# Linear attention on one core: two more groups' stores issued from SyncE instead of GpSimd

## The chip, the core and the metric

The kernel runs on one core of a Trainium2 chip. A core has TensorE (PE in the profile, with its weight loads as PEld), VectorE (DVE), ScalarE (ACT), GpSimd (POOL) and SyncE (SP), and sixteen DMA engines that carry out transfers between HBM and the core's SBUF. A transfer is issued by an instruction on one of the engines; here SP and POOL do it. The metric is the device time of one execution in microseconds, and the median over several executions is compared.

## What is computed

Q, K and V have the shape 8 × 12 × 512 × 64, in float32; the output has the same shape.

```python
Q_feat = np.maximum(0, Q) + 1
K_feat = np.maximum(0, K) + 1
KV = np.einsum('bhkd,bhkv->bhdv', K_feat, V)
K_sum = np.sum(K_feat, axis=2)
numerator = np.einsum('bhqd,bhdv->bhqv', Q_feat, KV)
denominator = np.einsum('bhqd,bhd->bhq', Q_feat, K_sum)
return numerator / (denominator[:, :, :, None] + 1e-10)
```

Each input is 12.58 MB, and so is the output. There are 96 heads; each has a 64 × 64 matrix KV and a vector K_sum.

## The kernel before

The 96 heads are cut into `NG` = 12 groups of eight heads. One group is 1 MB of each input in float32 and 1 MB of output. Loads convert to bfloat16 as they are written to SBUF (except the very first K load)[...]: one load per tensor for two groups at a time (`load_pair`, L105), except that the first and last two groups are loaded singly.

A group passes through these steps: `k_features` and `q_features` (VectorE), `v_blocks` (copies of V into a block layout, three on VectorE and one on ScalarE), `keys_values` (32 matmuls, then casts on ScalarE), `transposes` (16 on TensorE, copies on ScalarE), `output` (32 matmuls in two halves `h`, then on VectorE a reciprocal, L199, and a multiplication, L200, which writes `o_sb`), and `store` (L112). `o_sb` comes from a pool of `OUT_BUFS` = 6 buffers, so output 10 writes the buffer that store 4 reads, and output 11 that of store 5.

The order of the instructions on each engine is the order of the program text (`tc.manual_schedule`, L218). The loop of L234 runs over groups 0 to 10. In the turn of group g, VectorE prepares g, TensorE works on groups g−1, g−2 and g in turn, after odd groups the next loads are issued on POOL, and at the turn's end stands the store of group g − 3 (`LAG`, L16). So the loop issues stores 0 to 7. Behind the loop comes the rest of the work on the last groups, with outputs 9, 10 and 11, and at the very end (L257) the stores 8 to 11.

Before the change the stores of groups 0 to 9 are issued on POOL, one transfer of 1 MB each (L116). The stores of groups 10 and 11 are issued on SP, each as two transfers of 512 KB (L119), one for each half `h` that `output` writes. A transfer waits, on the engine that issues it, for the VectorE instructions that write its data. Apart from the four halves, SP issues one transfer only, the first load of K, at the start (L90).

Of the kernel before, what the change touches and what calls it, by code (L numbers as in the profile page):

```python
# [19 lines left out]
def kernel(  # L20
# [18 lines left out]
    nc = tc.nc  # L39
# [7 lines left out]
    NG = NPAIR // NP  # L47
# [64 lines left out]
    def store(g):  # L112
        o_sb = outs.pop(g)
        o_to = o_dram[:, g * NP : g * NP + NP]
        if g < NG - 2:
            nc.gpsimd.dma_start(out=o_to, in_=o_sb)  # L116
            return
        for h in range(2):
            nc.sync.dma_start(out=o_to[:, h:NP:2], in_=o_sb[:, h:NP:2])  # L119
# [98 lines left out]
    with tc.manual_schedule():  # L218
# [15 lines left out]
        for g in range(NG - 1):  # L234
            k_features(g)
            v_blocks(g)
            q_features(g)
            if g:
                transposes(g - 1)
            if g >= 2:  # L240
                output(g - 2)
            keys_values(g)
            if g % 2 and g // 2 + 2 < NG // 2:
                load_pair(g // 2 + 2)
            if g >= LAG:
                store(g - LAG)
# [10 lines left out]
        for g in range(last - LAG, NG):  # L257
            store(g)
# [30 lines left out]
```

## Time and profile before

| | |
|---|---|
| median of 8 runs | 127.59 us (127.2 to 128.22) |
| profiled execution | 127.59 us |
| its span, from the first to the last instruction | 125.8 us |
| busy: PE, DVE, ACT, POOL | 65.2, 88.1, 68.0, 27.8 us |
| granted TensorE clock, mean | 0.84 |
| stores issued on POOL | 10 of 1 MB |
| stores issued on SP | 4 of 512 KB |
| last VectorE instruction ends | 120.8 us |

Times in the profile are counted from the start of the span. In its rows, an arrow `out<-in` names the tile that is written and the one that is read, `xN` a count, and L116 a line of the kernel. The queue q0 (`software_dynamic`) holds the transfers issued on POOL, q1 (`hardware_dynamic`) those issued on SP; q8 and q14 are instruction fetches. Issuing a transfer is not the transfer: the profile shows the issue as an instruction, and separately when the transfer landed, as a semaphore that each of the sixteen DMA engines raises when its share is done. A share of the DMA queues can be a little over 100%, since an engine's packets overlap.

### The profile page before, as it was taken

The page shows a single profiled execution, that of the slowest core. Times are in us where ns is not written, and L with a number is a line of the kernel's source. Part 1 is how long each engine was busy: PE and PEld are TensorE (multiplying, and loading weights), DVE is VectorE, ACT ScalarE, POOL GpSimd, SP SyncE. Part 2 cuts the span into 40 slices and gives each one's busy share as a digit, 9 for nine tenths or more (in the row PEclk, how much of TensorE's full clock was granted, in tenths as well). Part 3 has the DMA queues.
Part 4 walks back from the last instruction along what each step waited for, and adds up shares of the span by engine and source line. Part 5 has one row for each costly group of instructions (what it writes and reads, how often), then busy time and mean ns, then how long its engine had stood idle before and what let it go on. Part 6 is the DMA issues. An engine that isn't in the chain of part 4 may idle for free.

```text
span 125.8 us, 2337 instructions
## 1 busy us (share of the span) xinstructions
PE 65.2 (52%) x960; PEld 48.4 (38%) x960; DVE 88.1 (70%) x188; ACT 68.0 (54%) x87; POOL 27.8 (22%) x43
## 2 busy tenths in 40 slices
PE   0005938000059785696929486004987659695500
PEld 0003636000046564574817364003656536483300
DVE  4896280206199799999989990519969999667930
ACT  7841396007600789729893962580069880988000
POOL 6990222000002082022800241202420202020000
PEclk9999999855555999679999999955589976999955
DMA  3999999999999999999999999999999999999992
GB/s 95 328 212 210 212 204 208 212 209 212 214 210 212 213 211 213 212 212 216 249 415 289 186 214 210 212 354 389 221 210 210 216 272 415 418 419 406 400 387 108
DMA packets 13419, 32.13 MB, mean 255 GB/s; under 512 B 608, under 2 KB 608, under 8 KB 13408
## 3 DMA queue, kind: packets, MB, share of 16 engines
q0 software_dynamic: 12048, 28.84, 98.5%
q1 hardware_dynamic: 1360, 3.15, 6.7%
q8 instruction: 7, 0.11, 0.3%
q14 instruction: 4, 0.03, 0.1%
HBM read 37.75 MB, written 12.58 MB: 400 GB/s over the span
## 4 chain that ended last, share of the span: by engine, by line
DMA 40%; DVE 26%; PE 17%; POOL 6%; issue 6%; DVEq 0%; POOLq 0%
DMA q_raw<-in_Q_dram 40%; DVE o_sb L200 15%; PE kva_ps L157 11%; DVE v_all L140 4%; PE qt_ps L176 3%; DVE recip L199 3%; PE o_ps L189 3%; POOL v_raw L99 2%; DVE qf L122 2%; DVE kf L122 2%; POOL q_raw L99 1%; POOL kva_diag L231 1%; POOL k_raw L99 1%; POOL identity masks.py:199 0%; POOL identity masks.py:197 0%
## 5 line engine op out<-in xcount | busy, mean ns | idle before, releaser
L157 PE MATMUL kva_ps<-v_all,kf 128*64 128x320 bf16 x384 | 36.4, 356 | 12.9 <-DVE v_all L140 12.9
L189 PE MATMUL o_ps<-kva_diag,qt 128*64 128x130 bf16 x384 | 19.3, 236 | 41.5 <-DVE o_sb L200 41.0
L140 DVE COPY v_all<-v_raw 32x2048 bf16<-32x2048 bf16 x36 | 26.4, 733 | 11.7 <-DMA v_raw<-in_V_dram 11.3
L200 DVE TENSOR_TENSOR o_sb<-o_ps,recip 128x512 f32<-128x512 f32 x48 | 33.2, 691 | 1.6
L157 PEld LDWEIGHTS <-kf 128*64 128x64 bf16 x384 | 25.4, 133 | 20.6 <-DVE v_all L140 13.1
L189 PEld LDWEIGHTS <-qt 128*64 128x64 bf16 x384 | 12.8, 115 | 47.1 <-DVE o_sb L200 45.3
L138 ACT COPY v_all<-v_raw 32x2048 bf16<-32x2048 bf16 x12 | 22.7, 1894 | 13.8 <-DMA v_raw<-in_V_dram 13.6
L177 ACT COPY qt<-qt_ps 128x1024 bf16<-128x1024 bf16 x24 | 29.7, 1310 | 0.3
L167 ACT CAST kva_diag<-kva_ps 64x256 bf16<-64x256 f32 x24 | 8.9, 371 | 33.2 <-PE kva_ps L157 33.0
L99 POOL DMA_DIRECT2D k_raw<-in_K_dram x7 | 5.3, 754 | 38.7 <-DVE kf L122 37.0
L122 DVE TENSOR_SCALAR qf<-q_raw 128x1024 bf16<-128x1024 bf16 x24 | 9.1, 422 | 6.4 <-DMA q_raw<-in_Q_dram 6.2
L116 POOL DMA_DIRECT2D out_dram<-o_sb x10 | 8.5, 849 | 22.3 <-DVE o_sb L200 13.0
L199 DVE RECIPROCAL recip<-o_ps 128x8 f32<-128x8 f32 x48 | 9.5, 198 | 4.9 <-PE o_ps L189 4.8
L122 DVE TENSOR_SCALAR kf<-k_raw 128x1024 bf16<-128x1024 bf16 x22 | 8.7, 437 | 6.0 <-DMA k_raw<-in_K_dram 6.0
L176 PE MATMUL qt_ps<-identity,qf 128*128 128x128 bf16 x192 | 12.8, 220 | 0.0
L176 PEld LDWEIGHTS <-qf 128*128 128x128 bf16 x192 | 10.8, 98 | 3.3 <-issue 3.1
L99 POOL DMA_DIRECT2D v_raw<-in_V_dram x8 | 6.1, 762 | 19.1 <-ACT v_all L138 10.9
L99 POOL DMA_DIRECT2D q_raw<-in_Q_dram x8 | 5.9, 742 | 4.2 <-DMA q_raw<-in_Q_dram 4.2
L213 DVE MEMSET v_all<- 128x3072 f32 (+1 forms) x2 | 4.4, 2192 | 1.1 <-DVE ones L225 0.7
L168 ACT CAST kva_diag<-kva_ps 64x4 bf16<-64x4 f32 x24 | 4.1, 169 | 0.0
L214 ACT COPY v_all<-zero 128x2048 f32<-128x2048 f32 x2 | 3.7, 1896 | 0.0
L214 ACT ACT_TABLE_LOAD x1 | 1.3, 1283 | 0.7 <-PEq L273 0.7
(12 smaller groups left out, 4.6 us busy)
## 6 DMA issues: line engine op xcount, KB each, us to landing
out_dram<-o_sb POOLq DMA_DIRECT2D x10, 1024.0 KB, 19.4
k_raw<-in_K_dram POOLq DMA_DIRECT2D x4, 1024.0 KB, 18.3
v_raw<-in_V_dram POOLq DMA_DIRECT2D x4, 1024.0 KB, 21.1
q_raw<-in_Q_dram POOLq DMA_DIRECT2D x4, 1024.0 KB, 25.3
v_raw<-in_V_dram POOLq DMA_DIRECT2D x4, 512.0 KB, 17.0
q_raw<-in_Q_dram POOLq DMA_DIRECT2D x4, 512.0 KB, 16.7
out_dram<-o_sb SPq DMA_DIRECT2D x4, 512.0 KB, 4.7
k_raw<-in_K_dram POOLq DMA_DIRECT2D x3, 512.0 KB, 23.5
```

Of the source, the lines that this page charges most:

```text
L99: nc.gpsimd.dma_start(out=t[:, ms], in_=drams[x][:, 2 * groups[0] : 2 * groups[-1] + 2])
L116: nc.gpsimd.dma_start(out=o_to, in_=o_sb)
L122: nc.vector.tensor_scalar(out=dst, in0=src, scalar1=1.0, scalar2=1.0, op0=ALU.add, op1=ALU.max)
L138: nc.scalar.copy(out=v_blk[g % 2][ps, b], in_=v_raw[ps])
L140: nc.vector.tensor_copy(out=v_blk[g % 2][ps, b], in_=v_raw[ps])
L157: nc.tensor.matmul(kva_ps[64 * n : 64 * n + 64], lhsT=kf[:, c, n, :], rhs=vb[:, :, n, c, :], start=(c == 0), stop=(c == C2 - 1),)
L167: nc.scalar.copy(out=kva[ps, :, n, 0:D], in_=kva_ps[ps, sb : sb + 4, :])
L176: nc.tensor.transpose(qt_ps[:, c, :], qf[:, half * C + c, :, :], identity)
L177: nc.scalar.copy(out=qt[:, :, :, half], in_=qt_ps)
L189: nc.tensor.matmul(ops[c // 4][64 * j : 64 * j + 64, c // 2 % 2, (c % 2) * W : (c % 2) * W + W], lhsT=qt[:, c, 32 * b : 32 * b + 32, :], r ...
L199: nc.vector.reciprocal(out=recip, in_=cells[:, :, :, :, D:D1])
L200: nc.vector.tensor_tensor(out=o_sb[:, h:NP:2, 4 * i : 4 * i + 4].rearrange("p n (b c) d -> p b c n d", b=2), in0=cells[:, :, :, :, 0:D], i ...
```

## The change

The stores of groups 8 and 9 are issued on SP instead of POOL, as one transfer of 1 MB each. Those of groups 0 to 7 stay on POOL. Those of groups 10 and 11 stay as they are, on SP in halves, and now stand behind stores 8 and 9 in SP's program. Nothing else is changed.

```diff
@@ -113,7 +113,7 @@
         o_sb = outs.pop(g)
         o_to = o_dram[:, g * NP : g * NP + NP]
         if g < NG - 2:
-            nc.gpsimd.dma_start(out=o_to, in_=o_sb)
+            (nc.gpsimd if g < NG - 4 else nc.sync).dma_start(out=o_to, in_=o_sb)
             return
         for h in range(2):
             nc.sync.dma_start(out=o_to[:, h:NP:2], in_=o_sb[:, h:NP:2])
```

## The prediction

> **What bounds the kernel now.** I began with the page's DMA rows, because the kernel moves much and computes little. The first row is the mean busy share of the sixteen DMA engines in forty slices; the two queue rows give packets, MB and the time of their packets as a share of sixteen engines' span; the last row is the traffic.
>
> ```profile
> DMA  3999999999999999999999999999999999999992
> q0 software_dynamic: 12048, 28.84, 98.5%
> q1 hardware_dynamic: 1360, 3.15, 6.7%
> HBM read 37.75 MB, written 12.58 MB: 400 GB/s over the span
> ```
>
> The DMA engines are at nine tenths or more from the second slice to the last but one. The page's chain of waits ends in VectorE work and doesn't show what happens behind it, so I followed the stores singly. The timeline (start, duration, queue, instruction) gives the issues of stores 8 and 9 on POOL and of the four halves on SP:
>
> ```profile
> 104.48 0.75 POOL L116 DMA_DIRECT2D out_dram<-o_sb  x1 [6.31 <-DVE o_sb L200]
> ...
> 111.92 0.75 POOL L116 DMA_DIRECT2D out_dram<-o_sb  x1 [6.69 <-DVE o_sb L200]
> ...
> 115.78 5.41 SPq L119 DMA_DIRECT2D out_dram<-o_sb  x4
> ```
>
> The DMA view, asked for short windows that hold one issue each, gives the us from issue to landing (last number). These are stores 4, 5, 8, 9, then the first and last half:
>
> ```profile
> out_dram<-o_sb POOLq DMA_DIRECT2D x1, 1024.0 KB, 19.3
> ...
> out_dram<-o_sb POOLq DMA_DIRECT2D x1, 1024.0 KB, 19.4
> ...
> out_dram<-o_sb POOLq DMA_DIRECT2D x1, 1024.0 KB, 12.9
> ...
> out_dram<-o_sb POOLq DMA_DIRECT2D x1, 1024.0 KB, 7.9
> ...
> out_dram<-o_sb SPq DMA_DIRECT2D x1, 512.0 KB, 5.3
> ...
> out_dram<-o_sb SPq DMA_DIRECT2D x1, 512.0 KB, 4.1
> ```
>
> Issue plus time to landing: store 4 lands at 107.3, 5 at 109.8, 8 at 117.4, 9 at 119.8, the halves from 121.1 to 124.9. They land in the order of issue at even distances. So the transfers stand in a queue, and a store's issue time says nothing about its landing.
>
> The trace keeps sixteen landing marks per transfer, one for each DMA engine. The last mark, that of the engine furthest behind, falls at 104.78 (the last load), 107.32, 109.82, 112.33, 114.83, 117.34, 119.86 (stores 4 to 9) and 121.13, 122.40, 123.65, 124.91 (the halves): steps of 2.51 us per MB and 1.26 per half, never a gap. The first mark of the same transfers runs 2.4 to 2.6 us ahead up to store 9 (117.36), then comes closer (118.72, 120.11, 121.72, 123.38). Cut at those last marks, the activity looks so (PE, PEld, DVE, ACT and POOL busy; then TensorE clock, DMA share, GB/s):
>
> ```profile
> 112.33:114.83 2.50, 1.84 (x36) 1.38 (x32) 0.81 (x2) 2.16 (x6) 0.35 (x1) 1.00 1.04 419
> 114.83:117.34 2.51, 1.25 (x24) 0.79 (x24) 2.41 (x7) 1.19 (x2) 0.00 (x0) 1.00 1.00 398
> 117.34:119.86 2.52, 1.25 (x24) 0.76 (x24) 2.42 (x7) 0.00 (x0) 0.00 (x0) 0.95 1.02 395
> 119.86:122.40 2.54, 0.00 (x0) 0.00 (x0) 0.89 (x3) 0.00 (x0) 0.00 (x0) 0.50 1.00 386
> 122.40:124.91 2.51, 0.00 (x0) 0.00 (x0) 0.00 (x0) 0.00 (x0) 0.00 (x0) 0.50 0.47 180
> ```
>
> Only the last row has idle DMA engines: those in front have run out of work while the last is still working off its backlog. So two clocks run to the end. The last data are ready at 120.79 (VectorE) and could land at 123.38, as they do on the front engine. The rear engine lands them at 124.91, and that sets the end: 124.91 + 0.91 of closing waits = the span, 125.82. The profiled execution is 127.59, so 1.77 lies around the span. 127.59 is also the median of the eight runs.
>
> **The change, part by part.**
>
> *POOL loses two issues*, 0.75 us each at 104.48 and 111.92. Behind them POOL has only its closing drain (111.90 to 121.26). Gain: 0. Nor do I count a quicker VectorE: its three block copies beside the first issue took 2.34 us against 2.15 to 2.17 at 79.91 and 89.54, but those had a POOL issue beside them too, and VectorE afterwards waits 1.07 us for PE (at 108.18). Were 0.19 us gained there, it would only bring data sooner to a rear engine that is late anyway.
>
> *SP gains two issues.* An SP issue is 0.37 us (halves) to 0.43 (the first K load, 1 MB). SP stood idle waiting for data for 114.7 us. Store 8's data are ready at 104.18, store 9's at 111.63, and the first half behind them on SP at 115.75: 4 us of room for an issue under half a microsecond. Nothing is delayed; cost 0. Between issue and first packet on SP's queue lie 1.2 us (issue 115.78, first packet 116.99), so store 8 can start at about 105.4. The rear engine then still has most of stores 4 to 7 to move (to 114.83); that backlog hides the latency, and it would cost 1.2 us per store if it were gone.
>
> *Bytes, and how they are cut.* POOL's stores went in packets of 4,096 bytes (160 ns each in the trace), SP's in 2,048 (84 ns). On the rear engine, stores 5 to 9 took 119.86 − 107.32 = 12.54, 2.508 per MB; four SP halves took 124.91 − 119.86 = 5.05, 2.525 per MB. Two stores change: 2 × 0.017 = **+0.03 us**.
>
> *Order.* How do two queues with work share an engine? The nearest rows are the DMA view of three stretches of 1 us after the first half had been issued:
>
> ```profile
> q0 software_dynamic: 84, 0.32, 80.4%
> q1 hardware_dynamic: 42, 0.09, 22.1%
> ...
> q1 hardware_dynamic: 126, 0.25, 67.4%
> q0 software_dynamic: 38, 0.12, 30.4%
> ...
> q1 hardware_dynamic: 192, 0.37, 97.1%
> q0 software_dynamic: 6, 0.02, 4.1%
> ```
>
> SP's queue (q1) grows only as engines run out of POOL's (q0): 22, 67, 97%. Store 9 landed 2.52 us after store 8, undelayed by the half beside it. The Trainium skill, "DMA: Bandwidth & Descriptors", section "Queues, rings and completion order", says otherwise: an engine takes turns, packet by packet, between the queues that have work. By that rule the rear engine would have alternated from 117.0, and store 9 would have landed 16 half-packets, 1.26 us, later than 119.86; it didn't. Perhaps what an engine has already taken in goes first. With a deeper backlog the turns may yet come, so I take both. By the row, stores 8 and 9 follow 4 to 7 as before: change 0. By the rule, store 8 goes between 4 to 7 and they land up to 2.5 us later, but the rear engine has the same sum of work and no gap: again 0 at the end.
>
> *What the delay could hit.* Six output buffers: output 10 writes store 4's (first write 114.23), output 11 store 5's (117.58). They are free at 107.32 and 109.82; with all of store 8 in front, at 109.8 and 112.3. Margins 4.4 and 5.3 us remain. The last load has its last mark at 104.78, before SP's first packet. PE and ACT are untouched.
>
> Sum: 0 + 0 + 0.03 + 0 = +0.03: span 125.85, time 127.62.
>
> What the trace doesn't show is an engine that really alternates between a POOL and an SP store. Below: the gaps of one queue filled by the other. POOL's stores ran at 419 GB/s; the section "Where 436 GB/s comes from" of the same page gives 435 as the ceiling. An estimate: 3.8% of the stretch shared by both queues (105.4 to 118.7, where store 9 would end) = −0.5 us. Above: a visit of a foreign packet. Instruction fetches are such visits; one of 16 KB took 0.96 us (3.0% of 16 engines in a 2 us window), though 16 KB of store cost 0.63 (four packets at 2,508/16 = 157 ns). That is 0.33 us over its bytes. Stores 8 and 9 bring 64 packets of 2 KB per engine; at one such surplus per 16 packets it is +1.3 us. I take 0, since the nearest row, POOL's and SP's stores at 117 to 119.9, runs on without a loss on the rear engine; both ends stay for the range.
>
> **Rivals.**
>
> *No change* (127.62, own range 127.3 to 127.95; chance 0.44). For it: the gapless rear engine, whose work is the same to 0.03 us. It covers the case that SP's stores really wait until POOL's are done, so that the change only relabels them.
>
> *Slower through alternation* (chance 0.32). Place: the rear engine, from 105.4 until POOL's four stores are through. Price: something per SP packet among POOL's. From 0.38/64 = 6 ns a packet it decides. At 10 ns: +0.64 + 0.03, about 128.3. For it: the fetch's surplus of 0.33 us. Against: an instruction fetch goes elsewhere than a store, and the stores seen together lost nothing.
>
> *Faster through two queues* (chance 0.24): the gaps fill, −0.5 + 0.03, about 127.1; or the spread of 2.5 us between front and rear engine shrinks, for which 124.91 − 123.38 = 1.5 us is all there is (126.1) before VectorE's end binds. For it: that engines wait at the end at all. Against: the same share of each store falls on each engine, whichever queue it goes by.
>
> A wait for an output buffer is a further way to lose, but its margin of 4.4 us makes it negligible; it is in the 0.32.
>
> **How the numbers follow.** About 0.3% (0.38 us) is what a measurement of this kernel can tell from no change; the eight runs spread from 127.2 to 128.22. Predicted is the first case, 127.62. The range takes in most of the other two: down to 127.0 (all the gaps filled), up to 128.6 (half of the upper bound and a bit); the spread shrinking altogether and a full fetch surplus are left out. Faster 0.24, same 0.44, slower 0.32.
>
> **What would show it.** Right: last marks on the rear engine still 2.5 us per MB to the end, last landing near 124.9, about 4.1 us after the last SP issue, which stays near 120.8. Order: if store 5 lands near 112, the queues take turns; if still near 109.8, they don't. Slower by alternation: the DMA engines' GB/s fall below 419 between 105 and 118. Faster: they rise, or the last half lands less than 4.1 us after its issue. I am wrong altogether if PE or VectorE end later than 120.8, or if a wait of VectorE for an output store appears.

## The result and the profile after

The changed kernel takes 127.87 us, the median of 19 runs (127.35 to 128.83); the kernel before takes 127.39 us in 54 runs (126.86 to 128.65). The ratio is 1.0042, with a 95% interval of 1.0025 to 1.0058: about half a microsecond slower. The profiled execution took 127.87 us, with a span of 126.1.

The page's DMA rows for the changed kernel look as before, with 2 MB moved from the first queue to the second:

```profile
DMA  3999999999999999999999999999999999999991
q0 software_dynamic: 11504, 26.74, 94.0%
q1 hardware_dynamic: 2416, 5.24, 10.9%
HBM read 37.75 MB, written 12.58 MB: 399 GB/s over the span
```

The traffic is the same and the DMA engines are as full. From issue to landing (last number, in us), in windows of the DMA view that hold one issue each, here are store 5, stores 8 and 9, then the first and the last half:

```profile
out_dram<-o_sb POOLq DMA_DIRECT2D x1, 1024.0 KB, 20.8
...
out_dram<-o_sb SPq DMA_DIRECT2D x1, 1024.0 KB, 13.0
...
out_dram<-o_sb SPq DMA_DIRECT2D x1, 1024.0 KB, 11.0
...
out_dram<-o_sb SPq DMA_DIRECT2D x1, 512.0 KB, 8.1
...
out_dram<-o_sb SPq DMA_DIRECT2D x1, 512.0 KB, 6.9
```

The last half waits 6.9 us, not 4.1, because VectorE ended at 117.79 in this execution, 3 us earlier than in that of before. That is not the change: in another execution of the same kernel (e1 below) it ended at 120.35, and the last landing came at 124.29. So in these executions the DMA backlog sets the end of the transfers, and not the end of VectorE.

The last marks on the rear engine are 104.06 (the last load), 106.67, 110.62, 114.36 and 118.48 (stores 4 to 7), 115.51 and 119.64 (8 and 9), then 120.89, 122.16, 123.41 and 124.70 (the halves). The two queues' work is interleaved, and **the last landing is not later than before, but 0.2 us earlier** (124.70 against 124.91). The loss comes after it. Here is the activity from the landing of POOL's last store, store 7, on, cut at last marks, with the columns of the prediction's table:

```profile
118.48:120.89 2.41, 0.00 (x0) 0.00 (x0) 0.00 (x0) 0.00 (x0) 0.00 (x0) 0.50 1.05 406
120.89:123.41 2.52, 0.00 (x0) 0.00 (x0) 0.00 (x0) 0.00 (x0) 0.00 (x0) 0.50 0.85 329
123.41:124.70 1.29, 0.00 (x0) 0.00 (x0) 0.00 (x0) 0.00 (x0) 0.00 (x0) 0.50 0.15 57
124.70:126.10 1.40, 0.00 (x0) 0.00 (x0) 0.00 (x0) 0.00 (x0) 0.00 (x0) 0.50 0.03 6
```

The last row, from the last landing to the end of the span, was this in the kernel before:

```profile
124.91:125.80 0.89, 0.00 (x0) 0.00 (x0) 0.00 (x0) 0.00 (x0) 0.00 (x0) 0.50 0.00 0
```

To the span's exact ends it is 1.40 us against 0.91: 0.49 more, about the loss measured. In this closing stretch no engine computes. The engines raise and await semaphores until all have arrived, and POOL clears them. Below are POOL's closing instructions in the view by source line, in windows that begin behind the last landing and end before the last two semaphore instructions: count, shortest/median/longest ns, and start of the first and of the last in us. First the kernel before, then the changed one:

```profile
L284 POOLq EVENT_SEMAPHORE  x2: 17/17/17, 125.1 to 125.2; - x2
L284 POOLq DRAIN  x2: 51/76/101, 125.2 to 125.5; - x2
L284 POOLq EVENT_SEMAPHORE_RANGE_CLEAR  x1: 135/135/135, 125.4 to 125.4; - x1
```

```profile
L284 POOLq EVENT_SEMAPHORE  x2: 17/17/17, 124.9 to 124.9; - x2
L284 POOLq DRAIN  x2: 45/144/244, 125.4 to 125.8; - x2
L284 POOLq EVENT_SEMAPHORE_RANGE_CLEAR  x1: 138/138/138, 125.6 to 125.6; - x1
```

A drain waits until POOL's own work is done; the long one ahead of the closing ends at 119.79 in the changed kernel, after POOL's last store has landed (118.48). Before, the first drain starts 0.06 us after the second semaphore instruction has ended (125.18 to 125.24 by the trace) and takes 101 ns. After, it starts 0.41 us after that instruction has ended (124.96 to 125.37) and takes 244 ns. Something is also new in the DMA view, an instruction fetch (q14) in the stretch from 125 to 127 us:

```profile
q14 instruction: 1, 0.01, 1.9%
```

Its packet starts at 126.08. In the kernel before no fetch starts after 118.1; one lies at 108.72, where POOL was waiting for store 9's data:

```profile
q14 instruction: 1, 0.01, 1.0%
```

This gives two theories. **A, the closing:** moving two stores off POOL shortened POOL's program, so that a boundary in it, at which the next block of instructions is fetched, moved out of a wait and into the closing. **B, alternation:** the DMA engines lose time when two queues take turns. For B speaks that the rear engine took 20.64 us from the last load to the end (104.06 to 124.70), against 20.13 before.

### The profile page after: what moved, and what is told of

Same layout as the page of the kernel before. It is cut to its first block, busy times and chain, and to the rows that moved or that the text cites. A ratio compares the mean times of both kernels' runs of the same rounds, so it can differ in the third digit from the quotient of the medians.

```text
span 126.1 us, 2336 instructions
## 1 busy us (share of the span) xinstructions
PE 66.3 (53%) x960; PEld 49.8 (40%) x960; DVE 87.9 (70%) x188; ACT 68.1 (54%) x87; POOL 26.5 (21%) x41
## 4 chain that ended last, share of the span: by engine, by line
DMA 39%; DVE 29%; PE 12%; POOL 6%; issue 6%; DVEq 0%; POOLq 0%
DMA q_raw<-in_Q_dram 39%; DVE o_sb L200 16%; PE kva_ps L157 8%; DVE v_all L140 5%; DVE recip L199 3%; PE qt_ps L176 2%; POOL v_raw L99 2%; DVE kf L122 2%; PE o_ps L189 2%; DVE qf L122 2%; POOL q_raw L99 1%; POOL kva_diag L231 1%; POOL k_raw L99 1%; POOL identity masks.py:199 0%; POOL identity masks.py:197 0%
## 5 line engine op out<-in xcount | busy, mean ns | idle before, releaser
L157 PE MATMUL kva_ps<-v_all,kf 128*64 128x320 bf16 x384 | 37.3, 362 | 12.7 <-DVE v_all L140 10.7
L157 PEld LDWEIGHTS <-kf 128*64 128x64 bf16 x384 | 26.7, 136 | 20.1 <-DVE v_all L140 12.8
L116 POOL DMA_DIRECT2D out_dram<-o_sb x8 | 7.1, 888 | 8.3 <-DMA out_dram<-o_sb 3.9
```

The costliest lines, as they stand in the source:

```text
L116: (nc.gpsimd if g < NG - 4 else nc.sync).dma_start(out=o_to, in_=o_sb)
L157: nc.tensor.matmul(kva_ps[64 * n : 64 * n + 64], lhsT=kf[:, c, n, :], rhs=vb[:, :, n, c, :], start=(c == 0), stop=(c == C2 - 1),)
```

## The experiments

They ran in three batches of four: e1 to e4 on one chip, the f and then the g runs on another. Each was compared with the kernel before in the same batch. "Closing" is the stretch from the last landing mark to the end of the span in the profiled execution.

**e1: the changed kernel again.**

> The changed kernel once more, for a second profile. Theory A (closing): the half microsecond comes after the last landing, in the closing instructions on POOL; from the last landing mark to the span's end it is 1.4 us again (0.9 before the change). Theory B (alternation): it comes from the DMA engines taking turns between two queues; the closing falls back to about 0.9 us and the rear engine's last landing is at 125.2 or later. The time is 127.9 by both.

Measured: 128.00 against 127.57 us, ratio 1.0036 (1.0006 to 1.0066); last landing 124.29, closing 1.41 us. B's landing at 125.2 or later isn't there.

**e2: two fillers at POOL's end.** `late` is a new tile of one column.

```diff
         for g in range(last - LAG, NG):
             store(g)
+        for _ in range(2):
+            nc.gpsimd.memset(late, 0.0)
```

> The changed kernel with two memsets of one column added on POOL behind its last store; they wait for nothing, so POOL is idle as long as in the changed kernel but has about as many instructions as before the change. Theory A, if the number of POOL's instructions decides: closing 0.9 us, time 127.4. Theory A, if POOL's long idleness decides: closing 1.4, time 127.9. Theory B: closing as in the repeat of the changed kernel, time 127.9.

Measured: 127.34 against 127.57 us, ratio 0.9984 (0.9957 to 1.0012); closing 0.92 us. The drains are short again:

```profile
L287 POOLq EVENT_SEMAPHORE  x4: 17/17/17, 125.0 to 125.7; - x4
L287 POOLq DRAIN  x3: 51/99/23902, 96.4 to 125.5; - x3
```

The longest of the three, 23.9 us from 96.4 on, is POOL's wait for its own stores, as long as in the changed kernel. So POOL was as idle as there, and idleness isn't the cause. More work, which nobody needs, makes the kernel faster by 0.66 us than the changed one beside it (128.00). The fetch now starts at 123.57, while POOL waits.

**e3: one late instruction on POOL.**

```diff
+        nc.gpsimd.tensor_copy(out=late, in_=outs[last][:, NP - 1, C - 1, D - 1 : D])
         for g in range(last - LAG, NG):
             store(g)
```

> The changed kernel with one copy of one column on POOL that waits for VectorE's last output, so POOL still has an instruction at about 118 to 121 us. Theory A, if POOL's idleness decides: closing 0.9 us, time 127.4. Theory A, if the number of instructions decides: one more is only half way, so 1.4 or 0.9. Theory B: time 127.9.

Measured: 127.75 against 127.57 us, ratio 1.0015 (0.9989 to 1.0040), which tells little; but the closing is 1.34 us, though POOL worked at 119.47. Its rows show more:

```profile
L286 POOLq EVENT_SEMAPHORE  x2: 17/17/17, 124.8 to 125.2; - x2
L286 POOLq DRAIN  x2: 51/98/144, 125.3 to 125.7; - x2
```

The gap now lies between the two semaphore instructions (124.8 to 125.2). One instruction more ahead of the closing has moved the gap to one instruction earlier in it. With two more it falls into the wait before the closing, which is e2.

**e4: half of the change.**

```diff
-            (nc.gpsimd if g < NG - 4 else nc.sync).dma_start(out=o_to, in_=o_sb)
+            (nc.gpsimd if g < NG - 3 else nc.sync).dma_start(out=o_to, in_=o_sb)
```

> Half of the change: store 9 alone goes to SP, store 8 stays on POOL. Theory B: half of the stretch with two queues or less, so at most half of the loss, 127.6. Theory A, if a single POOL instruction decides: either the whole loss (127.9, closing 1.4 us) or none (127.4, closing 0.9), not half.

Measured: 127.61 against 127.57 us, ratio 1.0014 (0.9982 to 1.0047), closing 0.92 us. The interval is too wide to tell half from none by the time; the closing says none. A store on POOL is two instructions in the trace, its wait and its issue, so this kernel has two more on POOL than the changed one, as e2 has.

**f1: the fillers at the start**, with `late` as in e2.

```diff
         nc.gpsimd.memset(zero, 0.0)
+        for _ in range(2):
+            nc.gpsimd.memset(late, 0.0)
         load_first_k()
```

> The changed kernel with the two memsets of one column at POOL's start, at about 1 us, instead of behind its last store. If the number of POOL's instructions ahead of the closing decides (a boundary in POOL's program that the change moved into the closing): closing 0.9 us, time 127.4, as with the two at the end. If what POOL does last decides (a closing right behind a store, or POOL idle since 97 us): closing 1.4, time 128.0.

Measured: 127.57 against 127.33 us, ratio 1.0011 (0.9981 to 1.0042); closing 0.91 us. The time lies between the two that were expected and decides nothing; the closing does. Where the fillers stand makes no difference to the closing; their number does.

**f2 and its repeat g3: the kernel before, with four POOL instructions fewer and no store moved.**

```diff
-    kva_diag = [const.tile([P, 4, 2, D1], BF16, name=f"kva_diag{i}") for i in range(NV)]
+    kva_all = const.tile([P, NV, 4, 2, D1], BF16, name="kva_diag")
+    kva_diag = [kva_all[:, i] for i in range(NV)]
...
-        nc.gpsimd.memset(zero, 0.0)
+        nc.vector.memset(zero, 0.0)
...
-        for t in kva_diag:
-            nc.gpsimd.memset(t, 0.0)
+        nc.vector.memset(kva_all, 0.0)
```

> The kernel before the change, with the stores where they were, but four instructions fewer on POOL: the three memsets of the block-diagonal tiles become one and go to VectorE with the memset of the zero column. If the number of POOL's instructions decides: closing 1.4 us, a gap of 0.4 us behind the second closing instruction on POOL, time 128.0 without any store moved. If the move of the stores decides: closing 0.9, time 127.5.

> The kernel before with four POOL instructions fewer, again, because its time was unclear (+0.2 us) while its closing was 1.4 us. By the boundary: closing 1.4, and 0.5 us more than the same kernel with four fillers, whatever it stands at against the kernel before, since its first microseconds differ.

Measured: closing 1.41 and 1.40 us. These are the rows of f2:

```profile
L284 POOLq EVENT_SEMAPHORE  x2: 17/17/17, 124.6 to 124.6; - x2
L284 POOLq DRAIN  x2: 51/144/238, 125.1 to 125.5; - x2
```

The gap is where the changed kernel has it, and the drain behind it takes 238 ns, with every store on its old queue. In time, f2 took 127.51 against 127.33 us, ratio 1.0016 (0.9990 to 1.0042), and g3 127.60 against 127.39, 1.0008 (0.9989 to 1.0027): less than the 0.5 us expected, and neither alone is told from zero. Both change the first microseconds too, so they needed their own reference:

**g4: the same with four fillers behind POOL's last store.**

```diff
         for g in range(last - LAG, NG):
             store(g)
+        for _ in range(4):
+            nc.gpsimd.memset(late, 0.0)
```

> The kernel before with those four POOL instructions moved or merged away and four memsets of one column added behind POOL's last store, so that POOL's count is that of the kernel before. By the boundary: closing 0.9 us and 0.5 us less than without the four. If the early memsets on VectorE are what lengthens the closing: closing 1.4 and the same time.

Measured: 127.31 against 127.39 us, ratio 0.9990 (0.9962 to 1.0018); closing 0.92 us. g3, beside it on the same chip, is 0.29 us slower, and its closing is 0.49 us longer. The direction is as expected. The size in the medians is smaller than in the closing; executions of one kernel differ by over 1 us, and by the profiles mostly in the time of the last landing (the changed kernel's three profiled executions, after, e1 and g1, took 127.87, 127.47 and 128.86 us, with last landings at 124.70, 124.29 and 125.66), so twelve executions of each don't settle such a rest.

**f5: the changed kernel with two POOL instructions fewer.** It merges the three memsets as f2 does, but leaves the one memset on POOL and `zero` as it was.

> The changed kernel with two POOL instructions fewer: the three memsets of the block-diagonal tiles become one over all three. If a boundary in POOL's program decides: the gap of 0.4 us comes two instructions later in the closing, closing 1.4, time 128.0. If POOL's first drain in the closing is slow for a reason of its own: the gap stays before that drain. If two instructions more or less cure it either way: closing 0.9.

Measured: 127.95 against 127.33 us, ratio 1.0056 (1.0031 to 1.0080); closing 1.45 us. The rows of its closing:

```profile
L284 POOLq EVENT_SEMAPHORE  x2: 17/17/17, 125.6 to 125.6; - x2
L284 POOLq DRAIN  x2: 108/150/193, 125.7 to 126.4; - x2
L284 POOLq EVENT_SEMAPHORE_RANGE_CLEAR  x1: 138/138/138, 125.9 to 125.9; - x1
```

The first drain is quick now (at 125.7, 108 ns). The gap comes behind the clearing, which ends at 126.00, and before the second drain at 126.4, which takes 193 ns instead of 51. Two instructions fewer have moved it to two instructions later. So no instruction of the closing is slow by itself.

**f6: the kernel before with two fillers at POOL's end**, the lines of e2.

> The kernel before the change with the two memsets of one column behind POOL's last store. If a boundary in POOL's program decides: it lay in a wait already, closing stays 0.9 and the time 127.5. If the memsets themselves help in some other way: closing below 0.9 or a time below 127.3.

Measured: 127.32 against 127.33 us, ratio 1.0007 (0.9987 to 1.0027); closing 0.91 us. The fillers don't help by themselves.

**g1 and g2: the changed kernel, without and with the two fillers of e2**, on one chip.

> The changed kernel a third time, beside the three others on one chip. By the boundary in POOL's program: closing 1.4 us, time 0.45 to 0.55 us over the kernel before and over the changed kernel with two fillers.

> The changed kernel with two memsets behind POOL's last store, again. By the boundary in POOL's program: closing 0.9 us, time as before the change within 0.25 us. If the first result was chance: nearer to the changed kernel than to the one before.

Measured: g1 127.86 against 127.39 us, ratio 1.0042 (1.0019 to 1.0065); g2 127.41, ratio 1.0015 (0.9985 to 1.0045). The closings, shown as the stretch from the last landing to the end in g1 and in g2:

```profile
125.66:127.09 1.43, 0.00 (x0) 0.00 (x0) 0.00 (x0) 0.00 (x0) 0.00 (x0) 0.50 0.02 6
```

```profile
124.33:125.25 0.92, 0.00 (x0) 0.00 (x0) 0.00 (x0) 0.00 (x0) 0.00 (x0) 0.50 0.00 0
```

In g1 the last landing itself came late, at 125.66, but so did the last load's last mark (105.42 against 104.06 in the other two executions of this kernel), before the first packet of SP's stores; the closing is as long as in those. The medians differ by 0.45 us here and by 0.66 us between e1 and e2; the closings by 0.51 and 0.48.

All profiles together, by the number of POOL instructions in the trace. Each has two fetch packets (q14) of 8,192 bytes after 100 us. One starts 2.0 to 3.1 us before VectorE's last instruction ends, in all fourteen; the table gives the other:

| kernels | POOL instructions | closing, us | gap | start of the fetch |
|---|---|---|---|---|
| f5 | 71 | 1.45 | before the second drain | 127.11 |
| changed, e1, g1 | 73 | 1.40, 1.41, 1.43 | before the first drain | 126.08, 125.69, 127.06 |
| f2, g3 | 73 | 1.41, 1.40 | before the first drain | 125.81, 125.87 |
| e3 | 74 | 1.34 | between the semaphore instructions | 125.92 |
| e2, g2, f1, e4 | 75 | 0.92, 0.92, 0.91, 0.92 | none | 123.57, 121.12, 121.00, 122.53 |
| before, g4 | 77 | 0.91, 0.92 | none | 108.72, 114.42 |
| f6 | 79 | 0.91 | none | 107.21 |

In all seven with a gap, it comes behind POOL's 68th instruction. With 75 instructions the 68th is the one before the closing's first semaphore, for which POOL waits anyway; in the kernel before and in f6 it is the issue of store 8, behind which POOL waits for store 9's data. In g4 it is the third of the four fillers, and there POOL had nothing to wait for but the filler before. Yet they follow each other without a gap (start, duration):

```profile
110.94 0.58 POOL L261 MEMSET late<- 128x1 f32 x4
```

So g4 has the fetch, 3.0 us behind that instruction, but no halt. The closings all fit A. That every pass of this point costs a halt is not shown.

The times agree when they are taken together. Of each batch's four versions two have the gap and two don't. The 72 executions with it took 0.40 us longer on average than the 72 without (95% interval 0.28 to 0.52, by resampling the executions). Among the versions with every store where it was, f2 and g3 against f6 and g4, it is 0.24 us (0.06 to 0.42): a loss without any store moved, of which the size is less sure.

**Alternation.** The changed kernel in the stretch from 107 to 108 us, by queue:

```profile
q0 software_dynamic: 70, 0.27, 66.1%
q1 hardware_dynamic: 70, 0.14, 36.9%
```

Seventy packets of each, and in every microsecond from 107 to 114 the two counts lie close together (67 to 75 from POOL, 64 to 75 from SP). Equal counts are what taking turns packet by packet gives; which engine took which packet isn't recorded, so a single turn can't be seen. What it costs is read over all sixteen engines, not from the rear one, which a fetch can hold back in one execution and not in another. The mean of the sixteen marks went from 103.33 (last load) to 118.67 (store 9) before, 15.34 us for the 6 MB of stores 4 to 9. In the changed kernel it went from 103.06 to 118.36 (store 9, the last of the six), 15.30 us. The seven other profiles with both stores on SP lie between 15.28 and 15.32 us, the four others with both on POOL between 15.30 and 15.39. So the turns cost no time that can be seen. Even on the rear engine the 20.64 us that spoke for B don't come again: it is 20.23 in e1 (104.06 to 124.29) and 20.24 in g1 (105.42 to 125.66), against 20.13 before. The 36 executions of e2, f1 and g2, which have the stores on SP and no gap, took 0.03 us more on average than the kernel before beside them (−0.12 to 0.20). B falls: **the move of the stores itself costs and gains nothing that these runs can tell**.

None of these versions beats the kernel before beyond its interval. For one who wants the stores on SP, the changed kernel with two fillers is the one that loses nothing measurable.

## Why the prediction was right, and where it was not

The time, 127.87 us, lies in the range given, but a quarter of a microsecond above the forecast of 127.62, and on the side that I had given 0.32. As a difference, "no change" was the likeliest case and didn't come: +0.03 us was predicted and +0.48 measured. The slower case came, by a way that I hadn't named. That 127.87 still lies near the forecast, and even in the range that I gave "no change" (to 127.95), is luck in part: the eight runs that I started from had their median at 127.59, 0.20 above the 127.39 of all 54, and the range was made for other causes.

*What bounds the kernel.* Right. The DMA engines stay full to the end, and an end of VectorE 3 us earlier moved the last landing by 0.2. The condition that I set the other way round, "the last SP issue stays near 120.8", was no good test, since that instant wanders from 117.7 to 120.4 between executions of the changed kernel.

*POOL loses two issues, "Gain: 0".* **This is the step that failed**, together with the 0.91 us of closing that the sum took over unchanged. I asked what work on POOL the two issues delayed and found none. I didn't ask what else depends on how many instructions POOL has. It cost +0.49 us by the closing (1.40 − 0.91), which is all of the measured +0.48 us (127.87 − 127.39).

*SP gains two issues.* Right in the cost, 0: nothing waits for SP, and the transfers began later than their data were there. The 1.2 us between issue and first packet was wrong: for store 8 it took 3.6 us (issue 102.52, first packet 106.11), in every run with that store on SP 3.5 to 3.7. The DMA engines were full all the while, so the delay cost nothing.

*Bytes, +0.03 us.* Not visible: 15.30 us for stores 4 to 9 against 15.34 in the mean of the engines.

*Order.* I put a row against the Trainium skill's rule, and with a deep backlog the packet counts agree with the rule. At 117 us before, SP's packets came only as POOL's ran out; with a deep backlog there are 70 and 70. The row showed the end of a backlog, where an engine seems to have taken in the rest of store 9 already (the 3.6 us that SP's first packet waited speak for it too, but this reading was not tested), and I took it for how the queues share. My test for it, store 5 near 112 or near 109.8, gave 110.62, and 109.66 and 112.75 in two more executions (e1 and g1); so it can't decide. Since I had reckoned both orders and found 0 for each, nothing hung on it. The output buffers had their margin: stores 4 and 5 landed at 106.67 and 110.62, the first writes of outputs 10 and 11 started at 111.22 and 114.58.

*The rivals.* Alternation was to cost up to 1.3 us or to gain 0.5; it did neither, and at 6 ns per packet or more (0.38 us) it would have shown in the 15.30 us. The spread of the last half's marks was 2.2 us (122.48 to 124.70), and 1.3 and 2.6 in e1 and g1, so that no shrinking is shown either.

## What to carry to other kernels

When a change takes instructions off an engine or adds some, look at the stretch between the last landing and the end of the span before explaining the difference by the work moved: half a microsecond can lie there. A difference of this size is tested by restoring the number of instructions with fillers, at a place where they cost nothing. And how a queue behaves at the end of a backlog doesn't tell how it behaves in the midst of one; give both a price, and ask whether the sum depends on it.

## What the runs showed of the hardware

POOL's program has a point, here behind its 68th instruction in the trace, at which it halts in the closing for 0.35 to 0.4 us more than usual. The next drain is then slow too (244 instead of 101 ns, 193 instead of 51; 144 in e3, where a semaphore instruction stands between). The point moves by one instruction in the closing for each one taken off or added before it, at the start or at the end, by whatever edit. A fetch packet of 8,192 bytes follows about 1.1 us after the halt begins (124.96 and 126.08 in the changed kernel, 126.00 and 127.11 in f5).

The Trainium skill, "Runtime: NRT & Kernel Launch", section "Instruction fetch mechanics", says that an engine's program is streamed to it in blocks, and that crossing a block's boundary is mostly hidden. That fits the six kernels in which POOL is waiting when it happens, and g4, in which it isn't and no halt is seen. In the closing it is not hidden, and it cost the kernel 0.4%. That the halt is this boundary is inferred from its moving with the count and from the packet that moves with it. Why the crossing shows in the closing and not among g4's fillers, why the packet is recorded after the halt, and what exactly POOL does in it, stays open.
